# S5 scans of a hybrid S5/SSD block in skewed order, step sizes transposed from SBUF, scans one job later

## The chip, the cores and the metric

The kernel runs on one core of a Trainium2 chip. The metric is the device time of one execution in microseconds (us); the kernel before has a median of 3029.45 us over three executions. TensorE does the matmuls, VectorE, ScalarE and GpSimd the elementwise work, and SP (SyncE) issues most of the DMAs; each engine takes its instructions in the order in which they stand in its queue.

## What is computed

One layer of a streaming encoder, in float32, for 1024 frames of 1024 channels: a half-weighted SwiGLU, a token mixer, another half-weighted SwiGLU and a norm. The mixer projects the normed input once and splits the result five ways; the part that matters here:

```
u_s5, z, xbc, dt_raw, gate_logits = split(h @ w_in)      # 1024, 2048, 4096, 32, 2048 columns
# S5: 64 groups of 16 channels, 64 complex states each
bu = einsum(u, B)                                        # per group
s[t] = a * s[t-1] + bu[t]                                # complex, over 1024 frames
y = Re(einsum(s, C)) + D * u;  g = gelu(y);  y_s5 = g * sigmoid(g @ w_glu + b)
# SSD: causal convolution of xbc, dt = softplus(dt_raw + bias), chunked scan, norm with z
merged = sigmoid(gate_s5) * (y_s5 @ w_ps5) + sigmoid(gate_ssd) * (y_ssd @ w_pssd)
x = x + merged @ w_out
```

## The kernel before

All tiles hold channels on 128 partitions and 512 frames (one half of the sequence) on the free axis. A float32 matrix product is made of three matmuls of rounded halves (`mm3`, L125 to L129): each weight tile is split into `whi` (ScalarE) and `wlo` (VectorE), each input into hh and hl.

The projection by `w_in` runs in **units** of 128 output columns and in **jobs**. The first four units of u (`plain`, L1269) and the step sizes (`ssd_dt_in`, L658) use ordinary products. Everything behind them goes by jobs of two units (`wino`, L324): seven **products** of twelve 128x512 matmuls each, with sums of weight tiles ws on GpSimd and of results ct on VectorE. Job kinds are u, z, g (gates), and x and b, whose results go through a causal convolution (`conv_direct`, tiles cv, four VectorE operations for a result and more at the seam). The list `first` holds fifteen jobs, "uuzz" then "zxzbzxzbzz" and "g": 105 products. `fill` gives them out one by one.

The **S5 scan** works on eight groups (ft) of 128 channels (`s5_scan`, L1171). A group's input part transposes uT (tiles pu, copied to uc), transposes again (pv, copied to U) and multiplies by win (psi). VectorE and GpSimd then make sp, the states ahead of each block of eight frames: four products with E, two sums, two scans (L1216, L1217), four products, two sums, all in tiles s5t. The output part multiplies U by K and sp by wo (py, copied to yc), transposes back (pg) and applies the gelu (gt), which goes to HBM as gD. `FILL` says how many products of `fill` stand between these steps: 1 behind pu, 1 behind pv, 5 behind psi, 2 behind py. `DTJOB` jobs (four) are done ahead of the scans. In this part TensorE's order is the order of the code (`manual_schedule`); the other engines and SP are ordered by a planner, by data and by free buffers. win, K, wo, E, uT have one buffer each, so a load waits for the last reader of the group before.

The **step sizes** dtT (two tiles of 32 x 512) are written to HBM as dtD (L677) early in the plain part, and `ssd_dt` (L679) loads them back (L688), transposes them (pt, L696) and turns them into decays with long chains of VectorE operations on tiles of 128 x 256 (dtv, spe, et, ek, dec); `dec` goes to HBM as cmD. `ssd_dt` has a high priority (`DTPRI`) and its transposes stand in TensorE's queue behind the fourth plain unit. Behind the first list of jobs comes the second, "xbxbgxbxbgxbxbg".

Of the kernel before, what the change touches and what calls it, by code (L numbers as in the profile page):

```python
# [15 lines left out]
L = 1024  # L16
KT = 8
NH = 2
# [13 lines left out]
DTJOB = 4  # L32
DTPRI = 800
FILL = 1, 1, 5, 2
# [31 lines left out]
class Block:  # L66
# [591 lines left out]
    def ssd_dt_in(self, h, rb, tp):  # L658
        nc, I = self.nc, self.I
        wd = self.wp.tile([128, 2 * TW], F32, name="wdt", tag="raw", bufs=2)[:, 0:256]  # L660
        nc.sync.dma_start(out=wd, in_=I["wdt"])
        whi = self.wp.tile([128, TW], F32R, name="wdth", tag="whi", bufs=3)[:, 0:256]
        nc.scalar.copy(whi, wd)
        wlo = self.wp.tile([128, TW], F32R, name="wdtl", tag="wlo", bufs=3)[:, 0:256]
        self.tt(wlo, wd, whi.bitcast(F32), ALU.subtract)
        dtT = []
        for hf in range(NH):
            ps = self.psA.tile([128, TW], F32, name=self.nm("psdt"), tag="a")
            for k in range(KT):
                c = slice(k * 32, (k + 1) * 32)  # L670
                self.mm3(ps[0:32, :], whi[:, c], wlo[:, c], h[hf][k][0], h[hf][k][1], k == 0, k == KT - 1)
            t = tp.tile([32, TW], F32, name=self.nm("dtT"), tag="ue", bufs=2)
            if hf:
                self.tt(t, ps[0:32, :], rb[hf][0:32, :], ALU.mult)
            else:
                nc.scalar.copy(t, ps[0:32, :])
            nc.sync.dma_start(out=self.dtD[hf], in_=t)  # L677

    def ssd_dt(self, cp):  # L679
# [3 lines left out]
        size = lambda nme: 512 if nme in ("dtT", "et", "ek", "eq", "eb") else 288 if nme == "spe" else 256  # L683
        self.tmp = tmp = lambda nme, n=512, dt=F32: cp.tile([128, size(nme)], dt, name=self.nm(nme), tag=nme,
                                                            bufs=2 if nme == "dtT" else 1)[:, 0:n]
        dtT = [tmp("dtT") for _ in range(NH)]
        for hf in range(NH):
            nc.sync.dma_start(out=dtT[hf][0:32, :], in_=self.dtD[hf])  # L688
# [5 lines left out]
        pt = self.psB.tile([128, TW], F32, name=self.nm("pt"), tag="b")  # L694
        for c in range(NCH):
            nc.tensor.transpose(pt[:, c * 32:(c + 1) * 32], dtT[c // 4][0:32, (c % 4) * 128:(c % 4 + 1) * 128],  # L696
                                self.ident[0:32, 0:32])
        v = tmp("dtv", n)
        r3 = lambda a: a.rearrange("p (c h) -> p c h", h=32)
        self.tt(r3(v), r3(pt[:, 0:n]), bc(par[:, 0:32], NCH, 1), A)  # L700
# [446 lines left out]
    def s5_load(self, ft, p):  # L1147
        nc = self.nc
        win = p.tile([128, 2, 512], F32, name=self.nm("win"), tag="win", bufs=1)
        nc.sync.dma_start(out=win, in_=self.winD[ft])  # L1150
        K = p.tile([128, 8, 128], F32, name=self.nm("K"), tag="K", bufs=1)
# [5 lines left out]
        E = p.tile([128, 2, 512], F32, name=self.nm("E"), tag="E", bufs=1)  # L1157
        nc.sync.dma_start(out=E, in_=self.eD[ft])
        uT = p.tile([128, L], F32, name=self.nm("uT"), tag="uT", bufs=1)
        nc.sync.dma_start(out=uT, in_=self.uD[ft])  # L1160
        return win, K, wo, E, uT

# [8 lines left out]
    def s5_scan(self, ft, recs, p):  # L1171
        nc, pe = self.nc, self.nc.tensor
        M, A, S = ALU.mult, ALU.add, ALU.subtract
        win, K, wo, E, uT = recs

        us = uT.rearrange("p (c j) -> p j c", j=8)
        uc = p.tile([128, L], F32, name=self.nm("uc"), tag="uc", bufs=2)
        for b in range(2):
            ps = self.psB.tile([128, TW], F32, name=self.nm("pu"), tag="b")
            for j in range(4):  # L1180
                pe.transpose(ps[:, j * 128:(j + 1) * 128], us[:, 4 * b + j, :], self.ident)
            nc.scalar.copy(uc.rearrange("c (g j m) -> c j g m", g=8, j=8)[:, 4 * b:4 * b + 4],
                           ps.rearrange("c (j g m) -> c j g m", j=4, g=8))
        yield FILL[0]
        U = p.tile([128, 8, 128], F32, name=self.nm("U"), tag="U", bufs=1)
        for b in range(2):
            ps = self.psB.tile([128, TW], F32, name=self.nm("pv"), tag="b")
            for g in range(4):
                gg = 4 * b + g
                pe.transpose(ps[:, g * 128:(g + 1) * 128], uc[:, gg * 128:(gg + 1) * 128], self.ident)  # L1190
            nc.scalar.copy(U[:, 4 * b:4 * b + 4, :].rearrange("p g c -> p (g c)"), ps)
        yield FILL[1]

        sin = []
        for i in range(2):
            ps = self.psB.tile([128, TW], F32, name=self.nm("psi"), tag="b")
            for q in range(4):
                for g2 in range(2):
                    pe.matmul(ps[64 * g2:64 * g2 + 64, q * 128:(q + 1) * 128],
                              lhsT=win[:, i, q * 128 + 64 * g2:q * 128 + 64 * g2 + 64], rhs=U[:, 2 * q + g2, :],  # L1200
                              start=True, stop=True)
            sin.append(ps)
        tl = lambda: p.tile([128, TW], F32, name=self.nm("s5t"), tag="s5t", bufs=S5T)
        Er, Ei = E[:, 0], E[:, 1]
        pr, t1, pi, t2 = tl(), tl(), tl(), tl()
        self.tt(pr, Er, sin[0], M)
        self.tt(t2, Ei, sin[0], M)
        self.tt(t1, Ei, sin[1], M)
        self.tt(pi, Er, sin[1], M)
        self.tt(pr, pr, t1, A, nc.gpsimd)  # L1210
        self.tt(pi, pi, t2, S, nc.gpsimd)
        m8 = tl()
        q3 = lambda a: a.rearrange("p (q c) -> p q c", q=4)
        self.tt(q3(m8), bc(self.mask01, 4, 1), bc(self.m8[:, 4 * ft:4 * ft + 4], 128, 2), M, nc.gpsimd)
        qr, qi = tl(), tl()
        nc.vector.tensor_tensor_scan(out=qr, data0=m8, data1=pr, initial=0.0, op0=M, op1=A)  # L1216
        nc.vector.tensor_tensor_scan(out=qi, data0=m8, data1=pi, initial=0.0, op0=M, op1=A)  # L1217

        sp_ = []
        for i in range(2):  # L1220
            s = p.tile([128, TW], F32, name=self.nm("sp"), tag="s5s", bufs=2)
            nc.gpsimd.memset(q3(s)[:, :, 0:1], 0.0)
            sp_.append(s)
        x1, x2 = tl(), tl()
        self.tt(x1, Er, qr, M)
        self.tt(x2, Ei, qi, M)
        self.tt(q3(sp_[0])[:, :, 1:128], q3(x1)[:, :, 0:127], q3(x2)[:, :, 0:127], S, nc.gpsimd)
        x3, x4 = tl(), tl()
        self.tt(x3, Er, qi, M)
        self.tt(x4, Ei, qr, M)  # L1230
        self.tt(q3(sp_[1])[:, :, 1:128], q3(x3)[:, :, 0:127], q3(x4)[:, :, 0:127], A, nc.gpsimd)
        yield FILL[2]

        yc = p.tile([128, L], F32, name=self.nm("yc"), tag="uc", bufs=2)
        ps = [self.psB.tile([128, TW], F32, name=self.nm("py"), tag="b") for _ in range(2)]
        for q in range(4):
            for g2 in range(2):
                pe.matmul(ps[g2][:, q * 128:(q + 1) * 128], lhsT=U[:, 2 * q + g2, :], rhs=K[:, 2 * q + g2, :],
                          start=True, stop=False)
            for i in range(2):  # L1240
                for g2 in range(2):
                    r = slice(64 * g2, 64 * g2 + 64)
                    pe.matmul(ps[g2][:, q * 128:(q + 1) * 128], lhsT=sp_[i][r, q * 128:(q + 1) * 128],
                              rhs=wo[r, i, q, :], start=False, stop=(i == 1))
        for g2 in range(2):
            nc.scalar.copy(yc.rearrange("c (j q e m) -> c e q j m", q=4, e=2, j=8)[:, g2],
                           ps[g2].rearrange("c (q j m) -> c q j m", q=4, j=8))
        yield FILL[3]
        gt = p.tile([128, L], F32, name=self.nm("gt"), tag="uc", bufs=2)
        for b in range(2):  # L1250
            ps = self.psB.tile([128, TW], F32, name=self.nm("pg"), tag="b")
            for j in range(4):
                pe.transpose(ps[:, j * 128:(j + 1) * 128], yc[:, (4 * b + j) * 128:(4 * b + j + 1) * 128], self.ident)
            nc.scalar.activation(gt.rearrange("p (c j) -> p j c", j=8)[:, 4 * b:4 * b + 4, :],
                                 ps.rearrange("p (j c) -> p j c", j=4), AF.Gelu_apprx_tanh)
        nc.scalar.dma_start(out=self.gD[ft], in_=gt)


    def pre_phase(self, h, rb, x, ctx, ctx2):
# [7 lines left out]
        self.dtD = self.dr.tile([NH, 32, TW], F32, name="dtD")  # L1267
# [11 lines left out]
        with self.pool("tbm", 1) as tb, self.pool("ftm", 1) as fp:  # L1279
            self.ssd_dt_in(h, rb, fp)  # L1280
            gen = self.prep(x, 1, h, rb, (1,), tb, wt)
            for u in range(UPLAIN):
                plain(u, fp)
                if u:
# [57 lines left out]
        with self.pool("cvm", 1, side="right") as self.cv, self.pool("wxm", 1) as wx:  # L1342
# [8 lines left out]
            with self.pool("s5m", 1, side="right") as p:  # L1351
                self.s5_consts(p)
                scan = (n for ft in range(8) for n in self.s5_scan(ft, self.s5_load(ft, p), p))
                with self.tc.manual_schedule(engines={mybir.EngineType.PE}):
                    for n in scan:
# [311 lines left out]
```

## Time and profile before

| | us |
|---|---|
| median of three executions | 3029.45 |
| lowest and highest | 3028.09, 3034.76 |
| the profiled execution | 3037.12 |
| its span, first to last instruction | 3035.3 |
| busy in the span: TensorE | 2817.8 |
| VectorE | 2266.4 |
| GpSimd | 1279.1 |
| ScalarE | 1138.1 |

The rows come from one profiled execution; times in them count from the first instruction. PE is TensorE, DVE VectorE, ACT ScalarE, POOL GpSimd; SPq is what SP's queue issues. A row's idle time in brackets is that of its engine just before it, with what ended it. The duration of a matmul in a row is that of its way through the array, and the next one starts before it ends: what a matmul costs is the distance to the next start. The plain units lie at 790 to 853 us, the jobs ahead of the scans at 860 to 944, the scans at 954 to 1285, the second list of jobs at 1298 to 1610.

### The profile page before, as it was taken

The page shows a single profiled execution, that of the slowest core. Times are in us where ns is not written, and L with a number is a line of the kernel's source. Part 1 is how long each engine was busy: PE and PEld are TensorE (multiplying, and loading weights), DVE is VectorE, ACT ScalarE, POOL GpSimd, SP SyncE. Part 2 cuts the span into 40 slices and gives each one's busy share as a digit, 9 for nine tenths or more (in the row PEclk, how much of TensorE's full clock was granted, in tenths as well). Part 3 has the DMA queues.
Part 4 walks back from the last instruction along what each step waited for, and adds up shares of the span by engine and source line. Part 5 has one row for each costly group of instructions (what it writes and reads, how often), then busy time and mean ns, then how long its engine had stood idle before and what let it go on. Part 6 is the DMA issues. An engine that isn't in the chain of part 4 may idle for free. (4 is left out here: it accounts for less than half of the span.)

```text
span 3035.3 us, 38489 instructions
## 1 busy us (share of the span) xinstructions
PE 2817.8 (93%) x13128; PEld 2260.1 (74%) x13128; DVE 2266.4 (75%) x3509; ACT 1138.1 (37%) x2065; POOL 1279.1 (42%) x1153
## 2 busy tenths in 40 slices
PE   6999799999988999899998899899999999999997
PEld 4787678778776777677776677678877888887776
DVE  6899996597897778789996767666245776666786
ACT  3322223444432444344444445334134333333443
POOL 5369863063323333333233676662111333332442
PEclk9999899999999999899999999999999999999998
DMA  2233343654134444323325676665343233335643
GB/s 103 88 122 132 118 163 104 222 185 134 63 103 138 150 146 148 103 90 112 104 91 180 226 223 194 212 213 196 97 156 115 83 112 111 104 103 173 201 131 104
DMA packets 208645, 421.65 MB, mean 139 GB/s; under 512 B 24001, under 2 KB 47937, under 8 KB 208449
## 3 DMA queue, kind: packets, MB, share of 16 engines
q1 hardware_dynamic: 187424, 374.64, 38.0%
q10 hardware_dynamic: 16416, 29.88, 2.7%
q0 software_dynamic: 4608, 14.68, 1.4%
q8 instruction: 103, 1.69, 0.2%
q14 instruction: 94, 0.76, 0.1%
HBM read 297.07 MB, written 122.04 MB: 138 GB/s over the span
## 5 line engine op out<-in xcount | busy, mean ns | idle before, releaser
L613 DVE TENSOR_TENSOR ct<-pw,ct 128x512 f32<-128x512 f32 x466 | 312.1, 684 | 195.0 <-PE pw L129 193.0
L129 PE MATMUL pw<-hh,wlo 128*128 128x512 f32 x1056 | 415.4, 394 | 19.5 <-DVE wlo L613 19.4
L127 PE MATMUL pw<-hh,whi 128*128 128x512 f32 x1056 | 418.9, 397 | 6.8 <-ACT whi L317 5.8
L128 PE MATMUL pw<-hl,whi 128*128 128x512 f32 x1056 | 414.2, 392 | 0.0
L127 PE MATMUL ps<-hh,whi 128*128 128x512 f32 x832 | 340.2, 410 | 18.6 <-ACT hh L207 5.9
L128 PE MATMUL ps<-hl,whi 128*128 128x512 f32 x832 | 336.3, 404 | 8.2 <-DVE hl L616 6.4
L129 PE MATMUL ps<-hh,wlo 128*128 128x512 f32 x832 | 333.4, 401 | 3.9 <-DVE wlo L121 3.9
L613 POOL TENSOR_TENSOR ws<-wraw 128x512 f32<-128x512 f32 x66 | 94.7, 1436 | 562.7 <-DMA wraw<-in_w_in 253.0
L129 PE MATMUL pw<-th,wlo 128*128 128x512 f32 x792 | 316.0, 399 | 14.0 <-DVE wlo L613 13.7
L127 PE MATMUL pw<-th,whi 128*128 128x512 f32 x792 | 316.0, 399 | 10.3 <-ACT whi L317 10.3
L128 PE MATMUL pw<-tl,whi 128*128 128x512 f32 x792 | 313.1, 395 | 0.0
L317 ACT CAST whi<-ws 128x512 fp32r<-128x512 f32 x264 | 163.3, 619 | 387.5 <-PE pw L128 247.4
L613 DVE TENSOR_TENSOR wlo<-ws,whi 128x512 fp32r<-128x512 f32 x264 | 224.0, 848 | 67.5 <-ACT whi L317 67.2
L128 PE MATMUL pd<-dal,whi 128*128 128x512 f32 x616 | 243.5, 397 | 11.9 <-DVE dal L613 11.9
L121 DVE TENSOR_TENSOR wlo<-wraw,whi 128x512 fp32r<-128x512 f32 x152 | 127.4, 840 | 169.7 <-ACT whi L119 162.9
L129 PE MATMUL pd<-dah,wlo 128*128 128x512 f32 x616 | 238.1, 400 | 16.3 <-DVE wlo L613 15.9
L129 PEld LDWEIGHTS pw<-hh,wlo 128*128 128x128 f32 x1056 | 199.6, 189 | 69.0 <-DVE wlo L613 27.2
L317 ACT CAST whi<-wraw 128x512 fp32r<-128x512 f32 x220 | 136.3, 619 | 284.7 <-PE pw L128 229.2
L127 PE MATMUL pd<-dah,whi 128*128 128x512 f32 x616 | 238.7, 393 | 2.0 <-ACT dah L135 2.0
L127 PEld LDWEIGHTS pw<-hh,whi 128*128 128x128 f32 x1056 | 200.3, 190 | 53.1 <-ACT whi L317 7.5
L128 PEld LDWEIGHTS pw<-hl,whi 128*128 128x128 f32 x1056 | 200.6, 190 | 40.6
L613 DVE TENSOR_TENSOR wlo<-wraw,whi 128x512 fp32r<-128x512 f32 x220 | 196.8, 895 | 40.2 <-ACT whi L317 39.6
(354 smaller groups left out, 6097.3 us busy)
## 6 DMA issues: line engine op xcount, KB each, us to landing
opDf<-ct SPq DMA_DIRECT2D x154, 256.0 KB, 2.3
wraw<-in_w_in SPq DMA_DIRECT2D x72, 512.0 KB, 3.6
dr<-opDf SPq DMA_DIRECT2D x70, 512.0 KB, 4.0
xbD<-cv SPq DMA_DIRECT2D x64, 256.0 KB, 2.0
xbc<-xbD SPq DMA_DIRECT2D x64, 256.0 KB, 4.4
e<-acD SPq DMA_DIRECT2D x64, 256.0 KB, 4.3
wraw<-in_f1up SPq DMA_DIRECT2D x22, 512.0 KB, 3.5
wraw<-in_f2gate SPq DMA_DIRECT2D x22, 512.0 KB, 3.5
```

The costliest lines, as they stand in the source:

```text
L121: nc.vector.tensor_tensor(out=lo, in0=r, in1=hi.bitcast(F32), op=ALU.subtract)
L127: t.matmul(ps, lhsT=whi, rhs=xhi, start=first, stop=False)
L128: t.matmul(ps, lhsT=whi, rhs=xlo, start=False, stop=False)
L129: t.matmul(ps, lhsT=wlo, rhs=xhi, start=False, stop=last)
L317: self.nc.scalar.copy(hi, src)
L613: (eng or self.nc.vector).tensor_tensor(out=out, in0=a, in1=b, op=op)
```

## The change

Three things change.

The step sizes stay in SBUF. `ssd_dt_in` returns its two tiles, which get buffers of their own; a new `ssd_dt_turn` transposes them between the second and third plain unit and copies the result to dtv, in a buffer of the pool rbp that the norms use; `ssd_dt` starts from that copy.

The scans are skewed. `s5_scan` runs over nine rounds: a round does the input part of group ft, starts its VectorE chain, and then does the output part of group ft - 1. U has two tiles for each group, in two places in turn (its own pool, and rbp); loads are split into uT, win, E ahead and K, wo (`s5_load_back`) behind. `FILL` becomes 2, 2, 2, 2, 1: two products behind each of pu, pv, psi and py, one behind pg.

`DTJOB` is 5: a z job more stands ahead of the scans.

```
-DTJOB = 4
+DTJOB = 5
-FILL = 1, 1, 5, 2
+FILL = 2, 2, 2, 2, 1
@@ ssd_dt_in
-            nc.sync.dma_start(out=self.dtD[hf], in_=t)
+            dtT.append(t)
+        return dtT
+    def ssd_dt_turn(self, dtT):
+        pt = self.psB.tile([128, TW], F32, name=self.nm("pt"), tag="b")
+        for c in range(NCH):
+            self.nc.tensor.transpose(pt[:, c * 32:(c + 1) * 32], dtT[c // 4][0:32, (c % 4) * 128:(c % 4 + 1) * 128],
+                                     self.ident[0:32, 0:32])
+        self.dtv = self.rbp.tile([128, TW], F32, name=self.nm("dtv"), tag="rbm", bufs=2)[:, 0:NCH * 32]
+        self.nc.scalar.copy(self.dtv, pt[:, 0:NCH * 32])
@@ ssd_dt
-            nc.sync.dma_start(out=dtT[hf][0:32, :], in_=self.dtD[hf])
-        self.tt(r3(v), r3(pt[:, 0:n]), bc(par[:, 0:32], NCH, 1), A)
+        self.tt(r3(v), r3(self.dtv), bc(par[:, 0:32], NCH, 1), A)
@@ s5_load, s5_load_back
+        nc.sync.dma_start(out=uT, in_=self.uD[ft])
         nc.sync.dma_start(out=win, in_=self.winD[ft])
+        nc.sync.dma_start(out=E, in_=self.eD[ft])
+        return uT, win, E
+    def s5_load_back(self, ft, p):
...
+        return K, wo
@@ s5_scan
+        back = None
+        recs = self.s5_load(0, p)
+        for ft in range(9):
+            if ft < 8:
+                uT, win, E = recs
...
+                yield FILL[0]
+                pool, tag, bufs = (self.rbp, "rbm", 2) if ft % 2 else (p, "U", 2)
+                Uh = [pool.tile([128, 4, 128], F32, name=self.nm("U"), tag=tag, bufs=bufs) for _ in range(2)]
...
+                yield FILL[1]
...
+                nc.vector.tensor_tensor_scan(out=qi, data0=m8, data1=pi, initial=0.0, op0=M, op1=A)
+                yield FILL[2]
+            if back:
+                U_, sp_, K, wo, f = back
...
+            if ft < 8:
...
+                self.tt(q3(sp[1])[:, :, 1:128], q3(x3)[:, :, 0:127], q3(x4)[:, :, 0:127], A, nc.gpsimd)
+                if ft < 7:
+                    recs = self.s5_load(ft + 1, p)
+            yield FILL[3]
+            if back:
...
+                nc.scalar.dma_start(out=self.gD[f], in_=gt)
+                yield FILL[4]
+            back = (U, sp, *self.s5_load_back(ft, p), ft) if ft < 8 else None
@@ pre_phase
                 plain(u, fp)
+                if u == 1:
+                    self.ssd_dt_turn(dtT)
-                for n in scan: ...
+                    for n in self.s5_scan(p):
```

In TensorE's queue the step sizes' transposes stood behind the last matmuls of the fourth plain unit (ps) and ahead of the first job (pw). Before:

```order
L128 MATMUL ps_7356<-hl_6680,whi_7351 128x512
L129 MATMUL ps_7356<-hh_6679,wlo_7353 128x512
L696 MATMUL pt_8114<-consts,dtT_8106 128x32 x4
L696 MATMUL pt_8114<-consts,dtT_8107 128x32 x4
L127 MATMUL pw_7505<-th_7244,whi_7506 128x512
L128 MATMUL pw_7505<-tl_7246,whi_7506 128x512
L129 MATMUL pw_7505<-th_7244,wlo_7508 128x512
```

Now they stand behind the second plain unit:

```order
L128 MATMUL ps_7177<-hl_6680,whi_7172 128x512
L129 MATMUL ps_7177<-hh_6679,wlo_7174 128x512
L684 MATMUL pt_7232<-consts,dtT_7071 128x32 x4
L684 MATMUL pt_7232<-consts,dtT_7098 128x32 x4
L127 MATMUL ps_7275<-hh_6529,whi_7267 128x512
L128 MATMUL ps_7275<-hl_6530,whi_7267 128x512
```

The eight transposes moved ahead by two plain units, and the first job follows the fourth unit directly.

In TensorE's queue, at the S5 groups, psi and py of one group had the same U, with five products (sixty matmuls pw) between. Before, at the second group:

```order
L1199 MATMUL psi_8691<-U_8660,win_8602 64x128 x8
L1199 MATMUL psi_8700<-U_8660,win_8602 64x128 x8
L127 MATMUL pw_8739<-th_7252,whi_8740 128x512
...
L129 MATMUL pw_8859<-th_7442,wlo_8862 128x512
L1238 MATMUL py_8878<-K_8604,U_8660 128x128
L1238 MATMUL py_8879<-K_8604,U_8660 128x128
L1243 MATMUL py_8878<-wo_8613,sp_8725 128x128
...
L1243 MATMUL py_8878<-wo_8613,sp_8727 128x128
```

Now py follows the next group's psi: at the third group's psi the U is another than at the py behind it, whose U, K and sp are the second group's:

```order
L1216 MATMUL psi_9200<-U_9117,win_8960 64x128 x4
L1216 MATMUL psi_9200<-U_9118,win_8960 64x128 x4
L1216 MATMUL psi_9209<-U_9117,win_8960 64x128 x4
L1216 MATMUL psi_9209<-U_9118,win_8960 64x128 x4
L127 MATMUL pw_9247<-hh_6529,whi_9248 128x512
...
L129 MATMUL pw_9265<-th_7450,wlo_9268 128x512
L1241 MATMUL py_9284<-K_9055,U_8780 128x128
L1241 MATMUL py_9285<-K_9055,U_8780 128x128
L1246 MATMUL py_9284<-wo_9064,sp_8944 128x128
...
L1246 MATMUL py_9284<-wo_9064,sp_8946 128x128
```

The use of sp moved behind the whole input part of the next group.

In SP's queue at the start of the scans the first uT was the last of the group's loads. Before, from the writing of dec (cmD) on:

```order
L755 DMA cmD<-dec_8189 128x512
L330 DMA wraw_8293<-in_w_in 128x1024
L1169 DMA m_8257<-m8D 128x32
L1331 DMA zD<-ct_7955 128x512
L1150 DMA win_8261<-winD 128x1024
L1154 DMA K_8263<-kD 16x8x128 x8
L1156 DMA wo_8272<-woD 128x1024
L1331 DMA zD<-ct_8051 128x512
L1158 DMA E_8274<-eD 128x1024
L1160 DMA uT_8276<-uD 128x1024
```

Now, from the same point on:

```order
L758 DMA cmD<-dec_8342 128x512
L1177 DMA m_8410<-m8D 128x32
L330 DMA wraw_8113<-in_w_in 128x1024
L1155 DMA uT_8414<-uD 128x1024
L1355 DMA zD<-ct_7963 128x512
L1157 DMA win_8416<-winD 128x1024
L1158 DMA E_8417<-eD 128x1024
L1166 DMA K_8716<-kD 16x8x128 x8
L1355 DMA zD<-ct_8059 128x512
L1168 DMA wo_8725<-woD 128x1024
```

uT moved ahead of win, E, K and wo, and the load of weights (wraw) ahead of it is that of the fifth job's second unit.

## Rows read from the trace of the kernel before

**Rows 1.** The page, part 1: busy time, share of the span, instructions of each engine
```profile
PE 2817.8 (93%) x13128; PEld 2260.1 (74%) x13128; DVE 2266.4 (75%) x3509; ACT 1138.1 (37%) x2065; POOL 1279.1 (42%) x1153
```

**Rows 2.** Table of stretches (us): busy time of each engine, granted clock, DMA
```profile
core 0: us, PE busy (x) PEld busy (x) DVE busy (x) ACT busy (x) POOL busy (x), PEclk, DMA share, GB/s
860.30:943.90 83.60, 81.76 (x349) 66.38 (x348) 80.20 (x141) 23.76 (x42) 22.43 (x19) 0.96 0.34 111
943.90:1298.70 354.80, 312.54 (x1756) 254.71 (x1757) 262.54 (x348) 133.86 (x222) 128.43 (x100) 0.92 0.43 137
1199.40:1250.40 51.00, 40.14 (x214) 32.28 (x213) 38.39 (x51) 17.00 (x29) 16.18 (x13) 0.83 0.36 116
1250.40:1285.00 34.60, 34.60 (x214) 28.49 (x213) 25.99 (x33) 14.22 (x25) 13.01 (x9) 1.00 0.33 109
1300.00:1610.00 310.00, 293.98 (x1261) 233.61 (x1260) 297.36 (x472) 141.25 (x251) 94.57 (x61) 1.00 0.29 100
```

**Rows 3.** TensorE's waits from 943.9 to 1298.7: total us, times, longest us
```profile
PE py L1243 <- POOL sp L613: 25.0, 7, 7.5
PE pu L1181 <- DMA uT<-uD: 10.5, 1, 10.5
PE pw L129 <- DVE wlo L613: 5.9, 5, 3.7
PE pv L1190 <- ACT uc L1182: 0.9, 2, 0.5
```

**Rows 4.** Timeline of TensorE, 943 to 956.5: start, us, instruction, [idle before <- releaser]
```profile
943.25 0.39 PE L128 MATMUL pw<-hl,whi 128*128 128x512 f32 x1
943.48 0.39 PE L129 MATMUL pw<-hh,wlo 128*128 128x512 f32 x1
954.32 1.94 PE L1181 MATMUL pu<-consts,uT 128*128 128x128 f32 x8 [10.45 <-DMA uT<-uD]
```

**Rows 5.** Timeline of TensorE, where the last group begins and where it ends
```profile
1250.48 1.06 PE L1181 MATMUL pu<-consts,uT 128*128 128x128 f32 x8
...
1285.07 0.48 PE L127 MATMUL pw<-hh,whi 128*128 128x512 f32 x1
```

**Rows 6.** Timeline of TensorE, behind the longest wait for sp
```profile
1243.53 0.63 PE L129 MATMUL pw<-hh,wlo 128*128 128x512 f32 x1
1243.96 0.63 PE L127 MATMUL pw<-hh,whi 128*128 128x512 f32 x1
```

**Rows 7.** Timeline of TensorE, 852.5 to 863
```profile
859.34 1.03 PE L696 MATMUL pt<-consts,dtT 32*128 32x32 f32 x8 [6.29 <-DMA dtT<-dtD]
...
862.62 0.80 PE L129 MATMUL pw<-th,wlo 128*128 128x512 f32 x1 [1.10 <-DVE wlo L613]
```

**Rows 8.** Timeline of VectorE, 855 to 863.5
```profile
857.49 0.17 DVE L705 COPY spe<-dtpar 128x32 f32<-128x32 f32 x1
860.41 0.42 DVE L613 TENSOR_TENSOR dtv<-pt,dtpar 128x256 f32<-128x256 f32 x1 [2.75 <-PE pt L696]
...
861.88 0.69 DVE L613 TENSOR_TENSOR wlo<-ws,whi 128x512 fp32r<-128x512 f32 x1
```

**Rows 9.** Timeline of SP's queue, 936 to 948 (DMAs that it issues)
```profile
936.25 0.32 SPq L755 DMA_DIRECT2D cmD<-dec  x1
...
939.26 6.38 SPq L1154 DMA_DIRECT2D K<-kD  x8
...
947.11 0.50 SPq L1160 DMA_DIRECT2D uT<-uD  x1
```

**Rows 10.** The tile s5t: duration ns min/median/max, first and last start us
```profile
L1216 DVE TENSOR_TENSOR_SCAN s5t<-s5t,s5t x8: 1208/2300/2312, 968.6 to 1262.5; 128x512 f32<-128x512 f32 x8
L1217 DVE TENSOR_TENSOR_SCAN s5t<-s5t,s5t x8: 1208/1211/1212, 972.0 to 1265.9; 128x512 f32<-128x512 f32 x8
```

**Rows 11.** Timeline of VectorE, 1005 to 1017
```profile
1011.17 2.29 DVE L1216 TENSOR_TENSOR_SCAN s5t<-s5t,s5t 128x512 f32<-128x512 f32 x1 [4.68 <-POOL s5t L613]
...
1015.69 0.68 DVE L613 TENSOR_TENSOR wlo<-ws,whi 128x512 fp32r<-128x512 f32 x1
```

More of the change, by code (lines that the diff above doesn't have):

```diff
@@ L671, in ssd_dt_in @@
                 self.mm3(ps[0:32, :], whi[:, c], wlo[:, c], h[hf][k][0], h[hf][k][1], k == 0, k == KT - 1)
-            t = tp.tile([32, TW], F32, name=self.nm("dtT"), tag="ue", bufs=2)
+            t = tp.tile([32, TW], F32, name=self.nm("dtT"), tag="dtT", bufs=2)
             if hf:
@@ L682, in ssd_dt @@
         n = NCH * 32
-        size = lambda nme: 512 if nme in ("dtT", "et", "ek", "eq", "eb") else 288 if nme == "spe" else 256
+        size = lambda nme: 512 if nme in ("et", "ek", "eq", "eb") else 288 if nme == "spe" else 256
         self.tmp = tmp = lambda nme, n=512, dt=F32: cp.tile([128, size(nme)], dt, name=self.nm(nme), tag=nme,
-                                                            bufs=2 if nme == "dtT" else 1)[:, 0:n]
-        dtT = [tmp("dtT") for _ in range(NH)]
-        for hf in range(NH):
-            nc.sync.dma_start(out=dtT[hf][0:32, :], in_=self.dtD[hf])
+                                                            bufs=1)[:, 0:n]
         par = tmp("dtpar", 64)
@@ L693, in ssd_dt @@
         tric, suf = cc[:, 0:128], cc[:, 128:256]
[L694 to L697, printed above, removed]
         v = tmp("dtv", n)
         r3 = lambda a: a.rearrange("p (c h) -> p c h", h=32)
-        self.tt(r3(v), r3(pt[:, 0:n]), bc(par[:, 0:32], NCH, 1), A)
+        self.tt(r3(v), r3(self.dtv), bc(par[:, 0:32], NCH, 1), A)
         e = tmp("spe", n + 32)
@@ L1148, in s5_load @@
         nc = self.nc
-        win = p.tile([128, 2, 512], F32, name=self.nm("win"), tag="win", bufs=1)
+        tile = lambda nme, shape: p.tile(shape, F32, name=self.nm(nme), tag=nme, bufs=1)
+        uT = tile("uT", [128, L])
+        nc.sync.dma_start(out=uT, in_=self.uD[ft])
+        win, E = tile("win", [128, 2, 512]), tile("E", [128, 2, 512])
         nc.sync.dma_start(out=win, in_=self.winD[ft])
+        nc.sync.dma_start(out=E, in_=self.eD[ft])
+        return uT, win, E
+    def s5_load_back(self, ft, p):
+        nc = self.nc
         K = p.tile([128, 8, 128], F32, name=self.nm("K"), tag="K", bufs=1)
@@ L1156, in s5_load @@
         nc.sync.dma_start(out=wo, in_=self.woD[ft])
[L1157 to L1161, printed above, removed]
+        return K, wo
     def s5_consts(self, p):
@@ L1169, in s5_consts, with s5_scan @@
         nc.sync.dma_start(out=self.m8, in_=self.m8D)
-    def s5_scan(self, ft, recs, p):
+    def s5_scan(self, p):
         nc, pe = self.nc, self.nc.tensor
         M, A, S = ALU.mult, ALU.add, ALU.subtract
[L1174 to L1197, printed above, removed]
-                for g2 in range(2):
[L1199 to L1256, printed above, removed]
@@ L1266, in pre_phase @@
         self.thD = self.dr.tile([16, NH, 128, TW], F32, name="thD")
-        self.dtD = self.dr.tile([NH, 32, TW], F32, name="dtD")
         def plain(u, fp):
@@ L1279, in pre_phase @@
         with self.pool("tbm", 1) as tb, self.pool("ftm", 1) as fp:
-            self.ssd_dt_in(h, rb, fp)
+            dtT = self.ssd_dt_in(h, rb, fp)
             gen = self.prep(x, 1, h, rb, (1,), tb, wt)
@@ L1352, in pre_phase @@
                 self.s5_consts(p)
-                scan = (n for ft in range(8) for n in self.s5_scan(ft, self.s5_load(ft, p), p))
                 with self.tc.manual_schedule(engines={mybir.EngineType.PE}):
-                    for n in scan:
+                    for n in self.s5_scan(p):
                         for _ in range(n):
```

70 lines of the change are left out of this document (added).

## Prediction

> **What bounds the kernel now.** I read the page first: TensorE is busy for 93% of the span [rows 1], far ahead of the others, so an idle microsecond of TensorE can be worth a microsecond of the span, and the question is where TensorE stands still. Next the table of stretches, for the part that the change touches [rows 2]. From 943.90 to 1298.70 us, the eight scans of the S5 branch, the mean granted clock is 0.92 and TensorE is busy for 312.54 of 354.80 us; in the 310 us behind it the clock is 1.00. VectorE is busy for 262.54 us of the scans, 74%. So TensorE is the bound there and it is not running at its best.
>
> The list of waits says what ended TensorE's idle time in that stretch [rows 3]: 25.0 us for the tiles sp (seven waits, up to 7.5), 10.5 us for the first uT, 5.9 us for weights wlo that VectorE makes, and 0.9 us for the copies uc: 42.3 us. The timeline gives the frame. TensorE's last matmul ahead of the scans starts at 943.48 and takes 0.39, so TensorE is free at 943.87; it goes on at 954.32 [rows 4]. The last group of channels begins with its transposes at 1250.48 and its last transposes end where the next matmul starts, at 1285.07 [rows 5]: 34.59 us, and the row of that stretch has TensorE busy throughout at a clock of 1.00 [rows 2]. I call this a clean group. The scans need 1285.07 - 943.87 = 341.2 us; eight clean groups would need 8 x 34.59 = 276.7. The difference, **64.5 us**, is the pool that the change can draw on: 42.3 us of it are the waits, and the remaining 22.2 us are matmuls at the lower of the two clock levels. At 1243.5 us two of them start 0.43 us apart [rows 6], against 0.23 at 943.25 [rows 4]: 1.2 GHz against 2.4. These follow the long waits; the group with the longest wait takes 51.0 us at a clock of 0.83 [rows 2].
>
> A smaller place lies ahead. TensorE waits 6.29 us, until 859.34, for the step sizes' way back from HBM, and shortly after 1.10 us more for the first product's wlo [rows 7].
>
> **The change, part by part.** *The amount of work.* Each group has the same matmuls as before and nine products of twelve matmuls between its parts (1+1+5+2 before, 2+2+2+2+1 after). So a clean group still costs 34.6 us; only waits and the clock can change. One job of seven products is done ahead of the scans and not after them, which moves no time by itself.
>
> *Step sizes (dtT).* The two writes and two loads through HBM go, and the eight transposes stand between plain units 1 and 2. They cost 0.96 us where they are (859.34 to 860.30) and cost that there too: zero. The 6.29 us wait goes, but what is late next is known: the first product needs a wlo, which VectorE starts at 861.88, three short operations behind dtv, which starts at 860.41 [rows 8]. But for a copy of 0.17 us at 857.49, VectorE had nothing ahead of dtv. What it did before that hangs on TensorE's last plain matmul, which now ends 1 us later: dtv can start at 858.5. From dtv to that wlo it took 1.47 us, and the new order has two more short operations there (0.17 and 0.30): wlo starts at 860.4. I take **-1.5 us**; if that gain is lost, 0; +1 if the transposes cost anew; if the whole wait were saved, -6.3.
>
> *The first uT.* Before, it stands in SP's queue behind the writing of dec (936.25), win, eight K transfers that take 6.38 us to issue, wo and E: issued at 947.11 [rows 9], and TensorE stands until 954.32. Now it stands third behind dec's write, ahead of win and K, and the scans begin a job later. dec's write itself hangs on VectorE's chain of exponentials and moves by no more than the 1.5 us above. So uT is issued at about 937, ten us earlier, and needed for its first two transposes about when TensorE has the first two matmuls of the fifth job done, near 943. Landing took 7.2 us at worst here (947.11 to 954.32); 937 + 7 = 944. So a remainder of 0 to 3 us; I take 1: **-9.5 us**, bounds -10.5 and 0 (if dec's chain comes as late as TensorE does).
>
> *The tiles sp.* They are made by VectorE and GpSimd from psi: four products, two sums, two scans, four more products, two more sums. Before, TensorE has five products between psi and the use (5 x 12 x 0.23 = 13.8 us), and waits seven times; the longest wait, 7.5 us, makes that path 21 us. Now the use of a group stands behind the whole input part of the next: ten or eleven products, some 28 to 30 us, and the S5 matmuls between them. So the waits go. What is left is the last group, where no next one follows: almost five products and the output part of the group before stand between, over 13.5 us, with the light products of a gate job on VectorE; before, the last group came without a wait in 13.8 beside such products. Behind the last output part only one matmul hides the copy yc, where two products did. The like copy uc, with one product (2.8 us) for cover, was still waited for by 0.5 us at most [rows 3], so a bare copy costs up to 3 us; I take 1.5. In all **-23.5 us** of 25.0; the near bound is half of it.
>
> *What is late next.* VectorE. Its 262.54 us of work now has to fit into about 290 us (the 354.8 of that stretch less the pool): 90%. Two rows show how TensorE fares beside such a VectorE: from 860.30 to 943.90 VectorE is busy 96% and TensorE idle 1.84 us of 83.60, 2.2%; from 1300 to 1610 VectorE is busy 96% and TensorE idle 16.0 of 310, 5.2% [rows 2]. On 276.7 us that makes 6 to 14 us. Now the waits for wlo and uc are 6.8. The longest, 3.7 us, came when a scan on VectorE waited 4.68 us for GpSimd's sum, with the wlo queued behind it [rows 11]; the new order has the same chain. uc and U get two products for cover and not one, so their 0.9 should go. I take 10, the middle, though 90% is below both, since the scans have more chains of this kind: **+3.2 us**, bounds -0.8 and +7.6.
>
> *The clock.* The 22.2 us follow the long waits. The stretch from 1300 on has 16 us of idle time in short pieces and a clock of 1.00 [rows 2], so short waits cost little of it. I leave 4 us: **-18.2 us**, bounds -22 and -11.
>
> Sum: -1.5 - 9.5 - 23.5 + 3.2 - 18.2 = **-49.5 us**. The profiled execution took 3037.12 us (span 3035.3 and 1.8 around it), 7.7 above the median of 3029.45; the stages behind keep their order on every engine, so the shift reaches the end. From the median: 3029.45 - 49.5 = **2980 us**.
>
> *A rule against it.* GpSimd's two sums per group overlap VectorE's scans: the first scan of a group has a median of 2300 ns, the second 1211 [rows 10]. The Trainium skill (GPSIMD Engine Reference, 8. Key points) says that GpSimd shares its SBUF interfaces with VectorE, with contention for instructions that have two SBUF inputs; the rows agree. By that page a denser schedule could stretch more of VectorE's operations, and if each second scan also took 2300 ns, VectorE would have 8 x 1.1 = 9 us more to do and the sum would be some 41 us. By the rows each GpSimd operation meets VectorE already, and their number does not change, so I add nothing.
>
> **The rivals.**
> 1. *All of the pool comes*: no new waits, 2.4 GHz throughout: 3029.45 - 64.5 - 1.5 = 2963. For it: the clean group of rows 5. Against it: that group had no convolutions on VectorE.
> 2. *VectorE's queue gives half back*: convolution jobs keep VectorE behind, a scan waits for GpSimd behind late weights [rows 11], and TensorE waits for wlo in place of sp, with the clock falling at some of them. Half of 25.0 + 6.8 + 22.2 = 27 is kept, and 11 from the first two parts: -38, 2991.
> 3. *The waits only move*: uT still waits for dec's chain, and wlo costs what sp did; half of the clock's loss and the step sizes stay as gain: -12.5, 3017.
> 4. *Slower*: SP's queue is in order, and it now carries loads that wait for TensorE (K and wo for the output part of the group before, uT and win for the input part) and for VectorE (E), ahead of the weights wraw. If weights come late in every group as sp did in the worst one, each costs 51.0 us: 8 x 51.0 = 408 against 341.2, +67 - 1.5: 3095. It decides from a mean group of 42.8 us on, 8.2 above a clean one. Against it: of TensorE's waits in rows 3 only the one of 3.7 us goes back to weights that came late.
> That the change does not do what it says is excluded by the order of TensorE's instructions, which has each output part behind the next group's psi.
>
> **How the numbers follow.** The forecast has 53%, rival 1 10%, rival 2 25%, rival 3 8%, rival 4 4%. The range reaches from the upper part of rival 1, 2966, past rival 2 to 3004, and leaves out most of rival 1's lower half, rival 3 and rival 4. A measurement of this kernel can tell about 0.2%, 6 us, from no change: faster has the first three and three quarters of rival 3, 94%; within 0.2% the rest of rival 3, 2%; slower 4%.
>
> **What would show it.** Right: no row of py waiting for sp but for the last group; pu's first wait under 3 us; no wait at pt, and the first product's wlo still waited for; groups of 35 to 37 us with a clock near 0.98; VectorE busy near 90% of the scans. Wrong: waits for wlo above 15 us in the scans, a clock still near 0.92, SP holding wraw behind K or E, or a stage from the next convolution jobs on that takes longer than the 310 us it takes now for the same rows.

## The result, and the profile after

The changed kernel takes 2977.64 us (median of four executions, 2970.88 to 2981.01) against 3028.77 for the one before on the same chip: a ratio of 0.983, 95% interval 0.981 to 0.985, or 51 us less. 2980 was forecast. The profiled execution took 2976.65 us, with a span of 2974.9.

Busy time of the engines, from the page, beside [rows 1]: the work is the same, but the matmuls take 25 us less.

```profile
PE 2793.0 (94%) x13128; PEld 2240.1 (75%) x13128; DVE 2264.5 (76%) x3509; ACT 1136.8 (38%) x2066; POOL 1280.6 (43%) x1153
```

The table of stretches of the changed kernel, beside [rows 2]: the jobs ahead of the scans, the scans, and the second list of jobs.

```profile
855.70:941.00 85.30, 81.98 (x351) 66.69 (x352) 80.28 (x144) 25.27 (x45) 22.25 (x20) 0.96 0.36 120
941.00:1249.60 308.60, 297.23 (x1767) 243.86 (x1765) 261.86 (x349) 129.93 (x222) 129.19 (x99) 0.99 0.50 156
1253.00:1552.00 299.00, 285.27 (x1214) 226.14 (x1214) 287.29 (x455) 135.43 (x242) 91.67 (x57) 0.99 0.29 99
```

The scans take 308.60 us where they took 354.80, with about the same matmuls (1767 and 1756). TensorE is idle for 308.60 - 297.23 = 11.4 us of them, not 42.3, and the granted clock is 0.99, not 0.92. VectorE does the same work (261.86 against 262.54 us) in less time: 85%. The second list keeps its pace: 1214 matmuls in 299.00 us, 4.06 for each us, as 1261 in 310 before.

TensorE's waits in that stretch, beside [rows 3]: none for sp or uT.

```profile
PE pw L129 <- DVE wlo L613: 6.3, 3, 3.0
PE pg L1274 <- ACT yc L1249: 4.4, 4, 1.8
PE psi L1216 <- ACT U L1207: 0.7, 2, 0.4
```

SP's queue at the start, beside [rows 9], and then TensorE's timeline, beside [rows 4]: uT is issued 1.6 us behind dec's writing and ahead of K's eight transfers, and its first transposes, at 941.00, follow without a wait. They are two of eight: the other six stand behind the fifth job, at 959.84, and wait for nothing either, so the fifth job lies inside the 308.60 us.

```profile
932.45 0.32 SPq L758 DMA_DIRECT2D cmD<-dec  x1
932.87 0.38 SPq L1177 DMA_DIRECT2D m<-m8D  x1
933.65 0.33 SPq L330 DMA_DIRECT2D wraw<-in_w_in  x1
934.04 0.42 SPq L1155 DMA_DIRECT2D uT<-uD  x1
...
936.01 8.46 SPq L1166 DMA_DIRECT2D K<-kD  x8
```

```profile
940.76 0.40 PE L128 MATMUL pw<-hl,whi 128*128 128x512 f32 x1
941.00 0.38 PE L1196 MATMUL pu<-consts,uT 128*128 128x128 f32 x2
941.13 0.47 PE L129 MATMUL pw<-hh,wlo 128*128 128x512 f32 x1
```

TensorE at the first job, beside [rows 7], and where the scans end. The 6.29 us wait for the step sizes is gone, but 3.49 + 2.77 us for the first product's whi and wlo stand there now. Behind the last pg the second list's first whi is late by 3.15 us, and matmuls at half rate follow (0.42 us apart).

```profile
851.87 0.39 PE L129 MATMUL ps<-hh,wlo 128*128 128x512 f32 x1
855.75 0.50 PE L127 MATMUL pw<-th,whi 128*128 128x512 f32 x1 [3.49 <-ACT whi L317]
859.25 0.79 PE L129 MATMUL pw<-th,wlo 128*128 128x512 f32 x1 [2.77 <-DVE wlo L613]
...
1248.71 1.09 PE L1274 MATMUL pg<-consts,yc 128*128 128x128 f32 x8 [0.72 <-ACT yc L1249]
1252.96 0.79 PE L127 MATMUL pw<-th,whi 128*128 128x512 f32 x1 [3.15 <-ACT whi L317]
1253.55 0.63 PE L128 MATMUL pw<-tl,whi 128*128 128x512 f32 x1
1253.97 0.63 PE L127 MATMUL pw<-hh,whi 128*128 128x512 f32 x1
```

**How far the shift reaches.** I cut each profiled execution at two matmuls that all kernels share: the last one of the fourth plain unit and the first transposes T of the SSD stage. Before, then after, in TensorE's timeline:

```profile
852.67 0.39 PE L129 MATMUL ps<-hh,wlo 128*128 128x512 f32 x1
...
1646.05 0.39 PE L802 MATMUL T<-xbc,xbc 128*128 128x128 f32 x2
```

```profile
1597.56 0.38 PE L805 MATMUL T<-xbc,xbc 128*128 128x128 f32 x2
```

From cut to cut it was 793.4 us and is 1597.56 - 851.87 = 745.7: -47.7 us. The step sizes' transposes now stand ahead of the first cut and cost 0.7 us there (the matmuls around them start at 828.54 and 829.47, where 0.23 is the distance without them), so the net is -47.0. A second profile of the changed kernel has 748.0 (after_again below): the stretch of one kernel repeats to some 2 us. What stands behind T is the same code, and took 3035.3 - 1646.05 = 1389.2 us before and 1377.3 after, 12 us less in this pair of profiles. No run ties that to the change (last section), and the medians, 51 us apart, contain less of it. "Stretch" below is the time from cut to cut.

### The profile page after: what moved, and what is told of

The parts are those of the page before. It is cut to its first block, busy times and chain, and to the rows that moved or that the text cites. A ratio compares the mean times of both kernels' runs of the same rounds, so it can differ in the third digit from the quotient of the medians.

```text
span 2974.9 us, 38461 instructions
## 1 busy us (share of the span) xinstructions
PE 2793.0 (94%) x13128; PEld 2240.1 (75%) x13128; DVE 2264.5 (76%) x3509; ACT 1136.8 (38%) x2066; POOL 1280.6 (43%) x1153
## 5 line engine op out<-in xcount | busy, mean ns | idle before, releaser
L129 PE MATMUL pw<-hh,wlo 128*128 128x512 f32 x1056 | 415.2, 394 | 20.7 <-DVE wlo L613 20.6
L127 PE MATMUL ps<-hh,whi 128*128 128x512 f32 x832 | 338.3, 408 | 17.6 <-ACT hh L207 6.2
```

What stands on the lines that cost most here:

```text
L127: t.matmul(ps, lhsT=whi, rhs=xhi, start=first, stop=False)
L129: t.matmul(ps, lhsT=wlo, rhs=xhi, start=False, stop=last)
```

## The experiments

**Each part alone, and all but the fifth job.** The first three are the kernel before with one part of the change, the fourth is the changed kernel with DTJOB = 4.

```
dt_alone     + dtT.append(t) ... + self.ssd_dt_turn(dtT) behind plain unit 1   (rest as before)
job5_alone   - DTJOB = 4    + DTJOB = 5                                        (rest as before)
skew_alone   + s5_scan, s5_load, s5_load_back, FILL of the changed kernel       (rest as before)
job4         - DTJOB = 5    + DTJOB = 4                                        (rest as changed)
```

> The kernel before with the step sizes' part alone (transposed from SBUF behind the second plain unit; scans and DTJOB as before). Theory: the 6.29 us wait ahead of the step sizes' transposes goes, the first product still waits for its weights wlo, so TensorE reaches the first job about 2 us earlier and nothing else changes: -2 us, with the first uT still waited for by about 10 us and sp by about 25. Rival: all of the 6.29 us comes, -6. Second rival: the shorter way of the step sizes also brings dec and so the first uT earlier, whose wait falls by several us: -8.

> The kernel before with DTJOB = 5 alone: a z job more ahead of the scans. Theory: uT is issued as before, some 11 us after dec is written, but is needed 19 us later, so its 10.5 us wait goes with the 1 to 3 us of half-rate matmuls behind it, and the waits for sp stay near 25: -12 us (-9 to -15). Rival (the waits only move): dec's chain or the loads come later with the job, and uT is waited for again: 0 to -3.

> The kernel before with the skewed scans and their split loads alone; step sizes through HBM and DTJOB = 4 as before. Theory: no wait for sp (25.0 before), the half-rate share falls from 22 to under 8 us, and uT, now ahead of K in SP's queue, lands nearly in time (0 to 3 us of wait): -45 us, mean granted clock of the scans 0.98 or more. Rival 1: the order of loads does not help and the fifth job was what saved uT: the wait for uT stays near 10 us, -35. Rival 2: skew alone moves the waits to VectorE's weights, over 15 us for wlo: -25.

> The changed kernel with DTJOB = 4. Theory: with uT ahead of win, E and K the fifth job has nothing left to give: a wait for uT of 0 to 3 us, and against that two products behind the last group's py, which hide its copy yc (0.72 us) and the weights of the next list's first product (3.15 us of wait in the changed kernel): within 4 us of the changed kernel, -50 us against the one before. Rival: the fifth job is needed for uT: its wait is 7 to 10 us again, and the kernel is 8 to 12 us slower than the changed one, -40.

| | median us | against before, 95% | stretch us |
|---|---|---|---|
| before | 3026.25 | | 793.4 |
| dt_alone | 3017.88 | 0.994 to 0.999 | 793.6 |
| job5_alone | 3010.82 | 0.993 to 0.998 | 774.1 |
| skew_alone | 2984.87 | 0.983 to 0.989 | 757.9 |
| job4 | 2993.36 | 0.985 to 0.991 | 761.0 |

*The skew* is the bulk: -35.5 us of stretch. No wait for sp is left, and uT is in time without the fifth job: pu at 941.99 has no wait. The new order of the loads is part of this run, and no run takes it apart from the skew; by the waits, 25.0 us were sp's and 10.5 uT's. The list of waits of skew_alone has 8.9 us for wlo where before had 5.9, short of rival 2:

```profile
PE pw L129 <- DVE wlo L613: 8.9, 4, 2.7
PE pv L1203 <- ACT uc L1194: 4.0, 2, 3.4
PE pg L1271 <- ACT yc L1246: 1.7, 1, 1.7
PE pw L127 <- ACT whi L317: 1.5, 1, 1.5
```

*The fifth job* is worth 10 to 15 us of stretch on top of the skew (761.0 or 757.9, against the changed kernel's 745.7 and 748.0), which neither theory gave for the reason named: in job4 uT is not waited for either. In its place whi is late by 3.78 us at the second product behind the first pu, and uc by 3.38 in the third group (pv at 1015.57; the second, in an expectation below, is a slip). The first goes back to SP's queue: in job4 the weights wraw are issued behind uT, win and E, GpSimd's sum ws waits for them until 939.49, and whi for ws. In skew_alone, with four jobs too, a wraw is issued at 935.70, ahead of uT at 937.04, and that whi is not waited for.

```profile
928.01 0.45 SPq L1155 DMA_DIRECT2D uT<-uD  x1
...
929.57 0.43 SPq L1158 DMA_DIRECT2D E<-eD  x1
930.10 0.54 SPq L330 DMA_DIRECT2D wraw<-in_w_in  x1
```

```profile
939.49 1.26 POOL L613 TENSOR_TENSOR ws<-wraw 128x512 f32<-128x512 f32 x1 [12.13 <-DMA wraw<-in_w_in]
```

```profile
942.79 0.50 PE L127 MATMUL pw<-th,whi 128*128 128x512 f32 x1 [3.78 <-ACT whi L317]
```

*Without the skew* the fifth job takes the wait for uT away, as expected, and gives more than the 12 us worked out (-15.4 by the medians, -19.3 of stretch), with the waits for sp falling as well, from 25.0 to 15.4 us. The edit doesn't touch sp's own chain; that other jobs now meet its steps is argued here, and job4_phase below tests it for the skewed kernel alone.

*The step sizes* give 2.6 us at their place (the first wlo ends its wait 7.4 us behind the start of the last plain matmul and not 9.95), of which the transposes ahead of the cut take back 0.7, and the wait for uT is 6.08 us, 4.4 shorter. By the last pg of the scans both are gone again: it starts 432.5 us behind the cut, and 431.6 before. The median says -8 us all the same. The span of the one profile is 10.7 us shorter, 5.8 of them ahead of the first cut and 5.1 behind T; the second is the same code, and the first spreads over 846.9 to 853.3 us in the fourteen profiles, with the step sizes' part and without. So the cause of the -8 us stays open.

**A longer chain of sp, before and after.** The same edit in both kernels: each of GpSimd's two sums for sp is done twice, with the same result.

```
  self.tt(q3(sp[0])[:, :, 1:128], q3(x1)[:, :, 0:127], q3(x2)[:, :, 0:127], S, nc.gpsimd)
+ self.tt(q3(sp[0])[:, :, 1:128], q3(x1)[:, :, 0:127], q3(x2)[:, :, 0:127], S, nc.gpsimd)      (and sp[1])
```

> The kernel before with GpSimd's two sums that end the chain of sp (about 1.5 us each) done twice, with the same result: the chain from psi to sp is 1.5 to 3 us longer in each group, TensorE's own work is as before. Theory (sp's chain sets the end of the groups): seven or eight groups pay 2 to 3 us each, the waits for sp rise from 25 to 40 to 48 us, and more of the matmuls behind them run at half rate: +15 to +30 us. Rival (sp's waits are a shadow of something else, such as VectorE's whole load): within 6 us of the kernel before.

> The changed kernel with the same two sums done twice. Theory: sp is ready 15 us or more ahead of its use, so the longer chain costs nothing: within 6 us of the changed kernel, no wait for sp but at most 3 us at the last group. Rival (the skew only just covers the chain, or GpSimd's longer work delays the weights ws and so TensorE): +10 or more, as waits for sp or for whi and wlo.

Before: 3069.76 us, +41.8 us (1.010 to 1.016). After: 2987.09 us, some 10 us above the changed kernel (2977.64 and 2976.41 in two other jobs). By the stretch it is +41.8 (835.2) and +7 to +9 (755.2). The waits in the scans, first of before_sp2, then of after_sp2:

```profile
PE py L1245 <- POOL sp L613: 54.8, 13, 8.7
PE pu L1181 <- DMA uT<-uD: 9.5, 1, 9.5
PE pw L129 <- DVE wlo L613: 4.6, 6, 1.8
```

```profile
PE pw L129 <- DVE wlo L613: 11.5, 5, 4.7
PE pg L1276 <- ACT yc L1249: 4.2, 5, 1.9
PE psi L1216 <- ACT U L1207: 1.1, 1, 1.1
PE pv L1206 <- ACT uc L1197: 0.3, 1, 0.3
```

The chain of sp did set the end of the groups before (25.0 us of waits became 54.8), and it doesn't now: no wait for sp. That is the mechanism of the change, shown. The price in the first was underestimated: in five of the eight groups TensorE waits for both tiles of sp one after the other, up to 0.97 + 8.68 us, and the added sums also slow VectorE, which has steps in the same chain; no run divides the 41.8 us between the two. The second was expected to be free and is not: the waits for wlo nearly double. The stretches of the changed kernel (in its second profile) and of after_sp2 say why:

```profile
938.40:1248.70 310.30, 296.53 (x1759) 243.10 (x1757) 260.37 (x349) 129.79 (x221) 129.33 (x99) 0.99 0.48 154
```

```profile
939.00:1255.10 316.10, 298.91 (x1759) 243.80 (x1757) 274.26 (x349) 129.70 (x220) 153.95 (x115) 0.98 0.49 151
```

VectorE has the same 349 operations and is busy 13.9 us longer (274.26 - 260.37) beside 16 more operations on GpSimd, and its weights come later. It stands idle for less time ahead of wlo<-ws (10.4 us against 17.6, for whi), so the sums ws are not what is late. Part of the price in both kernels is thus VectorE's; what only the kernel before pays, the waits for sp, is the chain's.

**Spacing without a skew, and more cover for yc.**

```
before_1161   - FILL = 1, 1, 5, 2       + FILL = 1, 1, 6, 1
after_22230   - FILL = 2, 2, 2, 2, 1    + FILL = 2, 2, 2, 3, 0
```

> The kernel before with FILL = 1, 1, 6, 1: one product taken from behind py and put behind psi, nothing skewed. Theory: each wait for sp gets 2.8 us shorter, 25 to about 9 us, but the copy yc is covered by one product only and is waited for by 0.5 to 2 us in each group, 4 to 12 us in all: -10 us. Rival 1: spacing alone is enough, -25 or better, and the skew is not needed. Rival 2: yc's waits take all of it, 0.

> The changed kernel with FILL = 2, 2, 2, 3, 0: the product behind pg put behind py, so that three products cover the copy yc. Theory: the waits of pg for yc, 4.4 us over four groups, go, and the half-rate matmuls behind them; pu follows pg at once and needs nothing from it: -4 us against the changed kernel (-1 to -7). Rival: ScalarE, which now has gt and uc back to back, brings uc or the weights whi late: no change or up to +6.

Spacing alone gives 3019.82 us against 3027.99 (0.995 to 0.999), -8 us and -11.0 of stretch. The waits for sp fall to 9.2 us as worked out. The 4 to 12 us expected for yc did not come (1.5); those for wlo rise from 5.9 to 11.6 in their place. The time is the theory's, the split of the waits is not, and spacing is no substitute for the skew.

The cover for yc brought nothing: 2984.11 us, 0.985 of before (0.982 to 0.988), not to be told from the changed kernel by the whole time, and its stretch is 4 to 6 us longer (752.1), as the rival had it. Only 1.2 us of wait for yc is left, at the last group, but where TensorE waited 1.51 us for yc it now waits 4.50 for a wlo:

```profile
1178.20 0.80 PE L129 MATMUL pw<-hh,wlo 128*128 128x512 f32 x1 [4.50 <-DVE wlo L613]
```

Two of the changed kernel's four waits for yc, 1.77 and 1.51 of the 4.4 us, were not a bare copy's time. In its ScalarE timeline the first of them stands behind th, which waits 3.40 us for VectorE's ct:

```profile
1131.60 0.63 ACT L1353 ACTIVATE th<-ct 128x512 f32<-128x512 f32 x1 [3.40 <-DVE ct L613]
1132.13 1.05 ACT L1249 COPY yc<-py 128x512 f32<-128x512 f32 x2
```

The second stands behind a step that waits 2.47 us for VectorE's cv. Of the other two, 0.38 us stands behind a step that waits for a DMA, and the last group's 0.72 is the copy itself. So where VectorE is late, a wait covered at one step came back at the next.

**The changed kernel again, without the step sizes' part, in phase with four jobs, and with a longer first list.** One chip for all four.

```
skew_job5    - dtT.append(t), ssd_dt_turn   + nc.sync.dma_start(out=self.dtD[hf], in_=t)
job4_phase   + DTJOB = 4,  first list "uuzz" + "xzbzxzbzz" + "gz"
after_x16    + ORDER = "uuzz" + "zxzbzxzbzz" + "gx", "bxbgxbxbgxbxbg", "gggg"
```

> The changed kernel as it is, on the same chip as the three others, so that differences of some 5 us among them can be told: 0.983 of the kernel before, 2977 us, waits in the scans of 10 to 13 us and none for sp, as in its first profile.

> The changed kernel without the step sizes' part (they go through HBM again). Theory: the 6.2 us wait ahead of the step sizes' transposes is back, the 6.3 us that the changed kernel waits for its first product's whi and wlo fall to 1.1, and the scans are as in the changed kernel: +2 us against it (0 to +4). Rival 1: dec and uT come later by the way through HBM, uT is waited for: +8. Rival 2: the step sizes' part costs something in the scans, and without it the kernel is faster by 4 or more.

> The changed kernel with DTJOB = 4 and the first z job behind the scans' z put to the end of the first list ("uuzz" + "xzbzxzbzz" + "gz"): one job less ahead of the scans, but each group of channels meets the same products as in the changed kernel. With DTJOB = 4 and the old list it was some 16 us slower, though uT was not waited for. Theory 1 (phase): what the fifth job changed is which convolutions meet which step of a group; then this kernel has the changed kernel's waits in the groups (wlo near 6, uc under 1) and is within 5 us of it. Theory 2 (lead): the S5 loads of the first groups stand ahead of the weights wraw in SP's queue when the scans begin a job earlier; then whi is waited for by 3 to 4 us behind the first pu and uc by 3 us in the second group again, and it stays 10 us or more slower.

> The changed kernel with the first convolution job of the second list appended to the first list, so that the last group's copy yc has two products beside it and six more follow. Theory: the 0.7 us wait for yc and the 3.15 us for the next list's first whi go, with some 3 us of half-rate matmuls behind them: -5 us against the changed kernel (-2 to -8). Rival: the wait for whi belongs to the start of the second list (its pools and weights), stays with it, and only yc's goes: 0 to -1.

| | median us | against before (3025.32), 95% | stretch us | behind T us |
|---|---|---|---|---|
| after_again | 2976.41 | 0.983 to 0.986 | 748.0 | 1377.6 |
| skew_job5 | 2983.41 | 0.985 to 0.988 | 748.5 | 1384.4 |
| job4_phase | 2985.21 | 0.986 to 0.989 | 749.5 | 1381.4 |
| after_x16 | 2984.41 | 0.985 to 0.988 | 748.3 | 1382.7 |

*skew_job5*: the wait at pt is back (6.11 us) and its first wlo is waited for by 1.10 us; at this place the step sizes' part gives 1.7 us (2.4, less the transposes' 0.7), near the 2 that were worked out. But the stretch is only 0.5 us longer, and most of the 7 us between the medians (6.8 in the profiles) lies behind T, in code that does not differ.

*job4_phase*: its groups have nearly the changed kernel's waits (wlo 7.5 us, none for uc, yc 6.2 against 5.4), and the whi behind the first pu is still late by 3.2 us. By the stretch theory 1 carries most: of job4's 13 us against after_again, 11.5 were the phase, by which convolutions meet which step; the lead is the small part. By the whole time neither theory came: its median is 8.8 us above after_again, where job4's was some 16 above the changed kernel; 3.8 of that are behind T.

*after_x16*: refuted. The wait for yc at the last group went and the stretch is no shorter: TensorE now stands 10.43 us at the start of the second list:

```profile
1281.13 0.80 PE L127 MATMUL pw<-th,whi 128*128 128x512 f32 x1 [10.43 <-ACT whi L317]
```

In ScalarE's queue the convolution's last steps stand ahead of that whi, and wait for VectorE themselves (an earlier one, at 1274.89, waited 2.04 us for a DMA):

```profile
1278.53 0.63 ACT L779 ACTIVATE ct<-cv 128x512 f32<-128x512 f32 x1 [2.83 <-DVE cv L616]
1279.97 0.58 ACT L365 COPY ct<-pw 128x512 f32<-128x512 f32 x1 [0.81 <-DVE cv L616]
1280.45 0.62 ACT L317 CAST whi<-ws 128x512 fp32r<-128x512 f32 x1
```

None of the versions beats the changed kernel.

## Why the prediction was right, point by point

- *What bounds the kernel.* Right: the pool of 64.5 us was there to be taken. The changed scans have all eight groups and 77.8 products, 5.8 more than eight clean groups, at 2.74 us each (12 matmuls of 0.228): 276.7 + 16.0 = 292.7. Of 308.6 us, 15.9 are left: 11.4 of waits and 4.5 at half rate. The pool shrank by 48.6; the four terms on it summed to 48.0.
- *Step sizes*: -1.5 forecast; -2.6 at the place, -1.9 with the 0.7 us that the transposes cost where they stand now. The first wlo was late next, as said, though with a late whi ahead of it.
- *First uT*: -9.5 forecast, -10.5 measured; the remainder of 1 us did not come. It was issued at 934.04 and not at 937, since dec's write moved by 3.8 us (936.25 to 932.45) where 1.5 were allowed. That the order of the loads was enough is shown by skew_alone.
- *sp*: -25.0 came in full, the last group too. The price of yc was mis-sized: 1.5 us at the last group were worked out; 0.7 came there and 3.7 in three other groups, 3.3 of them where ScalarE's queue puts yc behind steps that wait for VectorE. Together -20.6, not -23.5.
- *VectorE's waits*: 10 us taken, 7.0 came (wlo 6.3, U 0.7). VectorE is at 85%, not 90%: I divided its work by the stretch without the pool, but the stretch holds the rest of the pool too. The two misses, +2.9 for yc and -3.0 here, nearly cancel, and that is luck.
- *The clock*: -18.2 forecast, 4.5 - 22.2 = -17.7 measured. The run with longer waits agrees: from the first pu to the last pg the granted clock is 0.92 before, and 0.87 in before_sp2, with 54.8 us of waits for sp:

```profile
954.30:1285.00 330.70, 298.84 (x1695) 243.31 (x1696) 251.74 (x334) 125.45 (x211) 119.43 (x93) 0.92 0.42 134
```

```profile
952.60:1325.70 373.10, 311.47 (x1695) 252.13 (x1696) 263.24 (x334) 125.96 (x211) 145.97 (x109) 0.87 0.37 119
```

- *Not foreseen*: the 3.15 us at the second list (1.19 before), which take back 2 us; and that the fifth job works by phase. In the prediction it "moves no time by itself" and had only to bring uT in time; had uT's order been enough and phase nothing, job4 would have been as fast. The same terms would have given job4 about the same time; its stretch is 32 us shorter than before and skew_alone's 36, where the changed kernel's is 45 to 48. So 10 us or more came from a phase that the prediction had at nothing, and that the sum came so near is in part luck.
- *The rule of GpSimd and VectorE*, which I cited from the Trainium skill (GPSIMD Engine Reference, 8. Key points) and left at nothing: the change leaves VectorE's busy time as it was (261.86 against 262.54), and the scans have nearly the medians of [rows 10]:

```profile
L1231 DVE TENSOR_TENSOR_SCAN s5t<-s5t,s5t x8: 1207/2287/2309, 981.8 to 1225.5; 128x512 f32<-128x512 f32 x8
L1232 DVE TENSOR_TENSOR_SCAN s5t<-s5t,s5t x8: 1209/1211/2308, 985.2 to 1228.9; 128x512 f32<-128x512 f32 x8
```

  The rule itself holds here, and after_sp2 gives its size: 13.9 us of VectorE for 24.6 us of GpSimd. The weights wlo<-wraw,whi, with both inputs in SBUF, went from a mean of 837 ns to 1009; the results ct<-pw,ct, with one input in PSUM, stayed at 680.
- *Rivals.* The slower one had its mechanism at one place of job4, the second product behind the first pu (3.78 us), and not in every group. In the changed kernel, from the second group's psi, at 1002.85, to the eighth's, at 1220.95, a group takes 36.4 us in the mean, far below 42.8. Rival 2's sign, waits for wlo above 15 us, is absent.

## What to carry to other kernels

When a chain on other engines is longer than the work that an order puts between its start and its use, put the next piece's independent part between them: that alone gave 35.5 of the 47.7 us of stretch here, where more spacing gave 11. Then test the slack by doubling a step of the chain in both kernels; the waits in one pair of runs say whether the chain was the bound and whether it still is, while the time also holds what the doubled step does to other engines (7 to 10 us here with no wait for the chain). Count which work meets which step as well: one job more ahead of the scans was worth 10 to 15 us of stretch. A wait that ends on a copy may stand for a late engine two queues away, and covering it can move it on, as yc and the longer first list did.

## What the runs showed of the hardware

Work on GpSimd lengthens VectorE's: 16 sums more stretch the same 349 VectorE operations by 13.9 us (after_sp2), and the same 334 in the kernel before by 11.5 (251.74 to 263.24 us, in the two rows beside the clock above).

Code that no edit touches took from 1375.8 (skew_alone) to 1391.2 us (before_1161) behind T. One place of it is a run of 78 matmuls without any wait, 50 of a product and 28 of a norm's sums, before and then after:

```profile
2344.30:2361.80 17.50, 17.50 (x78) 14.85 (x77) 4.95 (x18) 2.78 (x5) 0.00 (x0) 0.80 0.13 47
```

```profile
2290.40:2304.70 14.30, 14.30 (x78) 12.33 (x78) 4.91 (x18) 2.83 (x5) 0.00 (x0) 1.00 0.15 53
```

The granted clock is 0.80 in the one, a mean of both levels, and 1.00 in the other. In both, 26 of the norm's matmuls stand in a row in the middle; before, the matmuls behind them start 0.43 us apart for some 5 us, and in the changed kernel 0.23. The two profiles of the changed kernel agree behind T (1377.3 and 1377.6), so this may belong to the kernel and not to chance; what sets it was not found. It puts differences of 5 to 8 us between whole times that no edit explains, and a small edit is better judged by its stretch.
